# A decoder block on one Trainium2 core: RWKV's bonus sum and gate product in rounded parts instead of plain fp32, with one buffer for a pair's low-rank weights

## The chip, the cores and the metric

The kernel runs as one program on one core of a Trainium2 chip. The metric is the time of one execution in device microseconds, and smaller is better. Five engines work side by side, each through its own instructions in a fixed order: TensorE (PE in the profile; its weight loads are listed apart as PEld), VectorE (DVE), ScalarE (ACT), GpSimd (POOL) and SyncE (SP, which here only issues transfers). An instruction whose operand or buffer is not ready waits, and everything behind it on the same engine waits with it.

## The reference

The reference is one residual block: parallel RWKV-7 time mixing and sliding-window attention, merged through gates, then a gated convolutional feed-forward part, on 512 tokens of width 2048. The change touches two lines of the RWKV part:

```
g = jax.nn.sigmoid(gd) @ g2
...
y = ((y - mu) * lax.rsqrt(var + GN_EPS)).reshape(B, S, RW_DIM)
y = y * gn_w.astype(f32) + gn_b.astype(f32)
bonus = jnp.sum(rh * kh * r_k.astype(f32), axis=-1, keepdims=True) * vh
out = (y + bonus.reshape(B, S, RW_DIM)) * g.astype(f32)
```

There are 16 heads of 64. `gd` has 256 columns, so the gate product sums over 256 values for each of the 1024 columns of `g`. The bonus sums `r*k*r_k` over the 64 values of a head.

## The kernel before

**Number formats.** A matmul on fp32 tiles is called plain here. The kernel's large products avoid it: `split` (L208 to L210) makes a rounded part `hi` with ACT (`AF.Copy` into the type float32r) and a rest `lo = src - hi` with DVE. A product is then a sum of passes over such parts. The rounded weights of the projections are made the same way in `load_w` (L232 to L246): one transfer into `raw`, `whi` on ACT (L240), `wlo` on DVE (L241). Both have four buffers, and each is used by 12 passes.

**Projection passes.** `project` (L248 to L257) runs three passes for each 128 rows of the sum: `whi*xhi` (L255), `whi*xlo` (L256) and `wlo*xhi` (L257), each 128x128 by 128x512 into the PSUM tile `acc`. One `ztile` is 48 such passes. They depend on nothing in RWKV's recurrence.

**The RWKV stage.** It works on eight pairs of heads, `p` = 0 to 7. `early(p)` makes the pair's keys, values and decays out of three projection tiles. `late(p)` runs the recurrence in eight chunks (passes `psG` L731, `psU` L734, `psS` L740, with copies between them on ACT and DVE) and then the group normalisation of `y` (DVE L758 to L765; its rsqrt is `rsqrt_small`, tiles `rg`, L193 to L200, thirteen small operations of which all but one use the one before). `final(p)` transposes `y` (L772), copies it back with ACT (L778), scales it, adds the bonus, multiplies by the gate product and stores it. The program calls `late(p)`, `early(p+1)`, `final(p)` and then three `emit_gate` projections. A scheduler then places the instructions of each engine by their dependences, so the projection passes of the next pair and of the gates stand between the passes of the recurrence. They are called fillers below.

**The two places of the change.** In `early(p)`, L589 makes `rk`, L591 multiplies it by the matrix `bo` (ones where two rows belong to the same head, zeros elsewhere) in one plain matmul, and L593 makes `bon` from the result. In `final(p)`, `lora(ps, ag, 1, 1 + NG)` runs two plain matmuls at L534, and L783 multiplies their sum into `yc`. The third use of `lora`, for `a2` in `early(p)`, is also listed under L534. `wl` (L537) holds a pair's low-rank weights in two buffers: 128 columns for the decay, 128 for `a2`, 256 for the gate. `ads` holds the right-hand sides of all `lora` products. PSUM results of all these products use the tag `bulk` with three buffers.

Of the kernel before, what the change touches and what calls it, by code (L numbers as in the profile page):

```python
# [8 lines left out]
F32 = mybir.dt.float32  # L9
F32R = mybir.dt.float32r  # L10
# [3 lines left out]
ALU = mybir.AluOpType  # L14
# [4 lines left out]
P = 128  # L19
S = 512  # L20
# [114 lines left out]
def block_kernel(ctx: ExitStack, tc: tile.TileContext, d: Dims, a: dict, out: bass.AP):  # L135
    nc = tc.nc
    act, dve, pool, pe, sync = nc.scalar, nc.vector, nc.gpsimd, nc.tensor, nc.sync
# [37 lines left out]
    K = {nm: cst[:, o - P : o - P + n] for nm, (o, n) in CONST_AT.items() if o}  # L175
# [7 lines left out]
    def col(nm, i=0):  # L183
        return pcol[:, PR[nm] + i : PR[nm] + i + 1]

    def rsqrt_small(pl, ss, scale, eps, mx=None, tag="rq"):
        n = ss.shape[-1]
        tl = [pl.tile([P, 8], F32, name=f"{tag}{i}", tag=f"{tag}{i}", bufs=2)[:, :n] for i in range(3)]
        v, y, t = tl
        if mx is not None:  # L190
            dve.tensor_scalar(v, ss, mx, None, op0=ALU.max)
        else:
            dve.tensor_scalar(v, ss, scale, eps, op0=ALU.mult, op1=ALU.add)  # L193
        dve.tensor_scalar(t.bitcast(I32), v.bitcast(I32), 1, None, op0=ALU.logical_shift_right)
        dve.tensor_scalar(y.bitcast(I32), t.bitcast(I32), -1, 0x5F3759DF, op0=ALU.mult, op1=ALU.add)
        dve.tensor_scalar(v, v, -0.5, None, op0=ALU.mult)
        for _ in range(3):
            dve.tensor_tensor(t, y, y, op=ALU.mult)
            dve.tensor_tensor(t, t, v, op=ALU.mult)
            dve.scalar_tensor_tensor(y, t, 1.5, y, op0=ALU.add, op1=ALU.mult)  # L200
        return y
# [6 lines left out]
    def split(hi, lo, src, pin=free):  # L208
        pin(act.activation(hi, src, AF.Copy))
        pin(dve.tensor_tensor(lo, src, hi.bitcast(F32) if hi.dtype == F32R else hi, op=ALU.subtract))  # L210
# [67 lines left out]
    if True:  # L278
# [3 lines left out]
        with tc.tile_pool(name="x0_ps", bufs=6, space=PSUM) as ps0:  # L282
            ssum = p0.tile([P, NT], F32, name="ssum")
            HT = NT // 2
            for h in range(2):
# [3 lines left out]
                r = rsqrt_small(p0, ssum[:, h * HT : (h + 1) * HT], 1.0 / d.D, RMS_EPS)  # L289
# [3 lines left out]
            for h in range(2):  # L293
                hs = slice(h * HT * P, (h + 1) * HT * P)
                for k in range(NK):
                    ps = ps0.tile([P, HT * P], F32, name="ps_x", tag="x")
# [45 lines left out]
        with ExitStack() as pt:  # L342
# [4 lines left out]
            def small():  # L347
                return mps.tile([P, S], F32, name="mi", tag="mi")
# [26 lines left out]
            for t in range(NKV):  # L375
# [12 lines left out]
                ps = small().rearrange("p (n c) -> p n c", c=P)  # L388
                for b in range(NT):
                    pe.transpose(ps[:, b], vf[:, b * P : (b + 1) * P], ident)  # L390
                ps = ps.rearrange("p n (h c) -> p n h c", c=HD)
# [14 lines left out]
            for g in range(NHK):  # L406
# [7 lines left out]
                for n in range(NT):  # L414
# [11 lines left out]
                    for h in range(GQ):  # L426
                        slope = float(2.0 ** (-8.0 * (g * GQ + h + 1) / d.HQ))
                        dve.scalar_tensor_tensor(sc[:, h, k0:], K["dist"][:, k0:], slope, scp[h % 2][:, h // 2, k0:],
                                                 op0=ALU.mult, op1=ALU.add)
# [17 lines left out]
                    for kb in kbs:  # L447
                        ps = small().rearrange("p (h c) -> p h c", c=P)
# [3 lines left out]
                    ps = small()  # L452
                    for kb in kbs:
                        for i in range(2):
                            pe.matmul(ps, vhl[:, n - 1 + kb, g].rearrange("p e c -> p (e c)"),
                                      phl[i][:, kb].rearrange("p h c -> p (h c)"),
                                      start=kb == kbs[0] and i == 0, stop=kb == kbs[-1] and i == 1)
                    ol = ap_.tile([HD, S], F32, name="ol", tag="ol", bufs=2)
                    act.activation(ol, ps[HD:P], AF.Copy)
                    ps, ol = (x[0:HD].rearrange("p (e j c) -> p e j c", e=2, c=P) for x in (ps, ol))  # L460
# [6 lines left out]
        with ExitStack() as pr:  # L467
            lp = pr.enter_context(tc.tile_pool(name="lora", bufs=1, reuse_waits="tile"))
            zp_ = pr.enter_context(tc.tile_pool(name="zpad", bufs=1, reuse_waits="tile"))
            bd = pr.enter_context(tc.tile_pool(name="bd", bufs=1, reuse_waits="tile"))  # L470
            wk = pr.enter_context(tc.tile_pool(name="wk", bufs=1, reuse_waits="tile"))
# [17 lines left out]
            def bulk():  # L489
                return blk.tile([P, S], F32, name="bulk", tag="bulk")  # L490

            NG = d.GL // P
            thw = lp.tile([P, S], F32, name="thw")
            ads = lp.tile([P, 1 + NG, S], F32, name="ads")
            acc = ztile(d.c_wd)
            shifted(acc, PR["muwd"], thw, 0)
            act.activation(thw, thw, AF.Tanh)
# [1 line left out]
                dve.memset(thw[d.DL : P], 0.0)  # L499
            dve.memset(thw[d.DL : d.DL + 1], 1.0)  # L500
            acc = ztile(d.c_ad)
            adz = ads[:, 0]
            shifted(acc, PR["muad"], adz, 1)
            if d.AL < P:
                dve.memset(adz[d.AL : P], 0.0)
            for i in range(NG):
                acc = ztile(d.c_gd + i * P)
                t = wtile("lw")
                shifted(acc, PR["mugd"] + i, t, i % 2)
                act.activation(t, t, AF.Tanh, scale=0.5)  # L510
                dve.tensor_scalar(ads[:, 1 + i], t, 0.5, 0.5, op0=ALU.mult, op1=ALU.add)

            HV = ((0, C), (C, P))

# [14 lines left out]
            def r3(ap, c=C):  # L529
                return ap.rearrange("p (n c) -> p n c", c=c)  # L530

            def lora(ps, w, lo, hi):
                for i in range(lo, hi):
                    pe.matmul(ps, w[:, i], ads[:, i], start=i == lo, stop=i == hi - 1)  # L534

            def early(p):
                wl = lp.tile([P, 2 + NG, P], F32, name="wl", tag="wl", bufs=2)  # L537
                sync.dma_start(wl, a["lora"][p].rearrange("p (k c) -> p k c", c=P))
                w2, ag = wl[:, 0], wl[:, 1:]

                acc = ztile(d.c_k + p * P)
                kz = wtile("kz")
                shifted(acc, PR["mu"] + NP + p, kz, 0)
                kk = wtile("kk")
                dve.tensor_scalar(kk, kz, col("k_k", p), None, op0=ALU.mult)
                sq = wtile("lg")
                act.activation(sq, kk, AF.Square)
                ps = bulk()
                head_stats(ps, sq)
                rs = rsqrt_small(wk, ps[:, 0 : 2 * NT], None, None, mx=1e-24)  # L550
                rb = head_rows(wk, bulk(), rs, "lg")
                dve.tensor_tensor(kk, kk, rb, op=ALU.mult)


                ps = bulk()
                for t in range(NT):
                    ts = slice(t * P, (t + 1) * P)
                    pe.matmul(ps[:, ts], thw[:, ts], w2, start=True, stop=True)
                lg = wtile("lw")
                act.activation(lg, ps, AF.Tanh, scale=0.5)  # L560
                dve.tensor_scalar(lg, lg, 1.0, None, op0=ALU.add)
                ps = bulk()
                for t in range(NT):
                    ts = slice(t * P, (t + 1) * P)
                    pe.matmul(ps[:, ts], lg[:, ts], K["tri"], start=True, stop=True)
                act.activation(Et[:, :, 1:], r3(ps), AF.Exp, scale=-0.5 * SQE)
                Ei = wtile("Ei")
                act.activation(Ei, ps, AF.Exp, scale=0.5 * SQE)

                ps = bulk()  # L570
                lora(ps, ag, 0, 1)
                ta = wtile("lw")
                act.activation(ta, ps, AF.Tanh, scale=0.5, bias=half[:, 0, p : p + 1])

                acc = ztile(d.c_r + p * P)
                rz = wtile("rz")
                shifted(acc, PR["mu"] + p, rz, 1)
                acc = ztile(d.c_v + p * P)
                vz = wtile("vz", 2)
                shifted(acc, PR["mu"] + 2 * NP + p, vz, 0)  # L580

                k2 = wtile("k2")
                dve.tensor_scalar(k2, ta, half[:, 1, p : p + 1], half[:, 2, p : p + 1], op0=ALU.mult, op1=ALU.add)
                dve.tensor_tensor(k2, k2, kz, op=ALU.mult)
                dve.tensor_scalar(ta, ta, 0.5, 0.5, op0=ALU.mult, op1=ALU.add)
                kb = kz
                dve.tensor_tensor(kb, kk, ta, op=ALU.mult)
                rk = wtile("lw")
                dve.scalar_tensor_tensor(rk, rz, col("r_k", p), k2, op0=ALU.mult, op1=ALU.mult)  # L589
                ps = bulk()  # L590
                pe.matmul(ps, K["bo"], rk, start=True, stop=True)  # L591
                bon = wtile("bon", 2)
                dve.tensor_tensor(bon, vz, ps, op=ALU.mult)  # L593
                return ag, Ei, kk, kb, k2, rz, vz, bon
# [173 lines left out]
            def final(p, st):  # L768
                ag, bon, y = st
                ps = bulk().rearrange("p (t c) -> p t c", c=P)  # L770
                for t in range(NT):
                    pe.transpose(ps[:, t], y[:, t * P : (t + 1) * P], ident)  # L772
                yc = wtile("gn")
                dst = yc.rearrange("p (t w c) -> p t w c", w=2, c=C)
                for w, (rl, rh) in enumerate(HV):
                    for h, (lo, hi) in enumerate(HV):
                        ol, oh = HV[1 - h]
                        act.activation(dst[lo:hi, :, w], ps[rl:rh, :, ol:oh], AF.Copy)  # L778
                dve.tensor_scalar(yc, yc, col("gn_w", p), col("gn_b", p), op0=ALU.mult, op1=ALU.add)
                dve.tensor_tensor(yc, yc, bon, op=ALU.add)  # L780
                ps = bulk()
                lora(ps, ag, 1, 1 + NG)
                dve.tensor_tensor(yc, yc, ps, op=ALU.mult)  # L783
                pool.dma_start(o_rw_d[p], yc)

# [80 lines left out]
    with ExitStack() as pbb:  # L866
# [8 lines left out]
        for m, i in order:  # L875
            hi, lo, r0, n, gi = parts[i]
# [11 lines left out]
            if second:  # L888
                w = min(XC, d.D)
                for e in range(m * XC, (m + 1) * XC, w):  # L890
                    t, c0 = divmod(e, d.D)
# [494 lines left out]
```

## Time and profile before

| | before |
|---|---|
| median of 3 runs | 2829.64 us (2828.12 to 2833.07) |
| profiled execution, its time | 2830.7 us |
| span of the profiled execution | 2828.9 us |
| granted TensorE clock, mean | 0.996 |
| instructions in the span | 45923 |
| HBM read and written | 554.38 MB and 174.40 MB |

The profiled execution's time is 1.8 us more than its span, which runs from the first to the last instruction. It lies 1.06 us above the median, inside the three runs. The RWKV stage runs from about 300 to 1110 us.

A row of the timeline begins with its start and its duration, both in microseconds. A bracket at the end gives the idle time before it and what ended that. Matmuls overlap, and their ends are modelled, so the distance between starts is what a pass takes in a dense row, not its duration. One plain matmul is recorded as two.

### The profile page before, as it was taken

The page shows a single profiled execution, that of the slowest core. Times are in us where ns is not written, and L with a number is a line of the kernel's source. Part 1 is how long each engine was busy: PE and PEld are TensorE (multiplying, and loading weights), DVE is VectorE, ACT ScalarE, POOL GpSimd, SP SyncE. Part 2 cuts the span into 40 slices and gives each one's busy share as a digit, 9 for nine tenths or more (in the row PEclk, how much of TensorE's full clock was granted, in tenths as well). Part 3 has the DMA queues.
Part 4 walks back from the last instruction along what each step waited for, and adds up shares of the span by engine and source line. Part 5 has one row for each costly group of instructions (what it writes and reads, how often), then busy time and mean ns, then how long its engine had stood idle before and what let it go on. Part 6 is the DMA issues. An engine that isn't in the chain of part 4 may idle for free.

```text
span 2828.9 us, 45923 instructions
## 1 busy us (share of the span) xinstructions
PE 2774.4 (98%) x17450; PEld 2403.0 (85%) x17450; DVE 1987.5 (70%) x3437; ACT 1342.1 (47%) x2256; POOL 225.1 (8%) x299
## 2 busy tenths in 40 slices
PE   7999999999999999999999899999999999999999
PEld 5777777777777777888888899999999999888887
DVE  4588677777777774545678777878787878655555
ACT  4355445444544553322465455555545555444444
POOL 0001000000000001011010011011101110000000
PEclk9999999999999999999999999999999999999999
DMA  7865766666666667878777789888988897877775
GB/s 216 227 159 163 187 167 168 175 164 158 175 162 171 160 165 223 234 248 292 237 251 211 210 235 241 229 229 227 241 236 222 228 242 228 315 245 241 256 256 190
DMA packets 223726, 607.04 MB, mean 215 GB/s; under 512 B 24448, under 2 KB 44560, under 8 KB 222480
## 3 DMA queue, kind: packets, MB, share of 16 engines
q1 hardware_dynamic: 156096, 432.64, 47.1%
q0 software_dynamic: 36064, 132.14, 24.5%
q10 hardware_dynamic: 31344, 39.31, 4.0%
q8 instruction: 137, 2.24, 0.3%
q14 instruction: 85, 0.70, 0.1%
HBM read 554.38 MB, written 174.40 MB: 258 GB/s over the span
## 4 chain that ended last, share of the span: by engine, by line
PE 87%; DVE 5%; ACT 3%; DMA 2%; issue 1%; SPq 0%; POOL 0%; ACTq 0%; DVEq 0%; POOLq 0%
PE X L1087 18%; PE X L954 11%; PE acc L256 9%; PE acc L255 9%; PE acc L257 9%; PE Y L954 9%; PE Y L1087 9%; PE Z L1087 4%; DVE wlo L241 1%; PE psS L740 1%; PE psG L731 1%; PE bulk L623 1%; PE bulk L673 1%; PE bulk L534 1%; ACT whi L240 1%
## 5 line engine op out<-in xcount | busy, mean ns | idle before, releaser
L255 PE MATMUL acc<-xhi,whi 128*128 128x512 f32 x1152 | 462.9, 402 | 1.9 <-DVE xlo L301 1.9
L257 PE MATMUL acc<-xhi,wlo 128*128 128x512 f32 x1152 | 463.8, 403 | 0.0
L256 PE MATMUL acc<-xlo,whi 128*128 128x512 f32 x1152 | 462.2, 401 | 0.0
L947 DVE TENSOR_TENSOR wlo<-raw,whi 128x1024 fp32r<-128x1024 f32 x210 | 256.9, 1224 | 205.1 <-ACT whi L946 204.9
L240 ACT ACTIVATE whi<-raw 128x512 fp32r<-128x512 f32 x352 | 220.0, 630 | 375.7 <-PE acc L256 295.1
L946 ACT ACTIVATE whi<-raw 128x1024 fp32r<-128x1024 f32 x210 | 222.8, 1061 | 290.6 <-PE X L954 152.9
L241 DVE TENSOR_TENSOR wlo<-raw,whi 128x512 fp32r<-128x512 f32 x352 | 241.3, 689 | 167.1 <-ACT whi L240 146.9
L1087 PE MATMUL X<-b,whi 128*128 128x256 f32 x1472 | 270.2, 284 | 2.3 <-DVE u L1107 0.9
L1087 PE MATMUL X<-t,whi 128*128 128x256 f32 x1408 | 259.6, 285 | 10.3 <-DVE u L1107 9.8
L1070 DVE TENSOR_TENSOR wlo<-raw,whi 128x1024 fp32r<-128x1024 f32 x176 | 215.0, 1222 | 77.6 <-ACT whi L1069 77.3
L1087 PE MATMUL Y<-t,whi 128*128 128x256 f32 x1408 | 257.1, 283 | 0.0
L255 PEld LDWEIGHTS acc<-xhi,whi 128*128 128x128 f32 x1152 | 217.6, 189 | 43.4 <-issue 2.5
L256 PEld LDWEIGHTS acc<-xlo,whi 128*128 128x128 f32 x1152 | 217.5, 189 | 41.9 <-issue 3.3
L257 PEld LDWEIGHTS acc<-xhi,wlo 128*128 128x128 f32 x1152 | 217.5, 189 | 38.3 <-issue 1.1
L1069 ACT ACTIVATE whi<-a 128x1024 fp32r<-128x1024 f32 x132 | 139.3, 1056 | 216.5 <-DVE a L1063 214.3
L1087 PEld LDWEIGHTS X<-b,whi 128*128 128x128 f32 x1472 | 230.7, 193 | 3.1 <-issue 2.4
L1087 PEld LDWEIGHTS X<-t,whi 128*128 128x128 f32 x1408 | 221.6, 194 | 10.9 <-DVE u L1107 7.2
L1087 PEld LDWEIGHTS Y<-t,whi 128*128 128x128 f32 x1408 | 219.8, 192 | 0.0
L1087 PE MATMUL X<-b,wlo 128*128 128x256 f32 x736 | 209.3, 284 | 2.1 <-DVE wlo L1070 2.1
L1070 DVE TENSOR_TENSOR wlo<-a,whi 128x1024 fp32r<-128x1024 f32 x132 | 161.7, 1226 | 67.3 <-ACT whi L1069 66.7
L1087 PE MATMUL X<-t,wlo 128*128 128x256 f32 x704 | 200.4, 285 | 0.0
L1087 PE MATMUL Y<-t,wlo 128*128 128x256 f32 x704 | 199.4, 283 | 0.0
(339 smaller groups left out, 5762.1 us busy)
## 6 DMA issues: line engine op xcount, KB each, us to landing
raw<-in_w_up_dram SPq DMA_DIRECT2D x180, 512.0 KB, 4.6
raw<-in_w_z_dram SPq DMA_DIRECT2D x288, 256.0 KB, 3.9
s_dn<-in_w_dn_dram POOLq DMA_DIRECT2D x88, 512.0 KB, 5.9
raw<-in_w_up_dram POOLq DMA_DIRECT2D x88, 512.0 KB, 8.7
raw<-s_dn SPq DMA_DIRECT2D x88, 512.0 KB, 3.8
raw<-in_w_dn_dram SPq DMA_DIRECT2D x66, 512.0 KB, 3.5
a<-in_w_up_dram SPq DMA_DIRECT2D x48, 512.0 KB, 6.9
s_dn<-in_w_dn_dram SPq DMA_DIRECT2D x44, 512.0 KB, 4.9
```

What stands on the lines that cost most here:

```text
L240: act.activation(hi, raw, AF.Copy)
L241: dve.tensor_tensor(lo, raw, hi.bitcast(F32), op=ALU.subtract)
L255: pe.matmul(acc, whi[:, j], xhi[:, k], start=first, stop=False)
L256: pe.matmul(acc, whi[:, j], xlo[:, k], start=False, stop=False)
L257: pe.matmul(acc, wlo[:, j], xhi[:, k], start=False, stop=last)
L534: pe.matmul(ps, w[:, i], ads[:, i], start=i == lo, stop=i == hi - 1)
L946: act.activation(whi, wr, AF.Copy)
L947: dve.tensor_tensor(wlo, wr, whi.bitcast(F32), op=ALU.subtract)
L954: pe.matmul(dst, l[:, q, ts], r[:, es], start=fst and j == 0, stop=lst and j == 2, skip_group_check=True)
L1069: pin(act.activation(hi, t, AF.Copy))
L1070: pin(dve.tensor_tensor(lo, t, hi.bitcast(F32), op=ALU.subtract))
L1087: pin(pe.matmul(ps, l[:, k], r[:, k], start=start and k + i == 0, stop=last and i == 2, skip_group_check=True))
```

## The change

The bonus product is taken as two passes over float32r tiles. `rk` is split into two parts, `bo` is copied once into a float32r tile `bor`, and the two parts are multiplied one after the other into the same PSUM tile. The tiles for the parts are the existing work tiles with the tags `lg` (rounded part) and `gn` (rest), one buffer each. The first also holds `sq` and `rsb` in `early`, the second the squares in `late` and `yc` in `final`.

The gate product is taken as six passes in place of two plain matmuls: for each of the two halves of 128, rounded by rounded, rounded weights by the rest of the data, rest of the weights by rounded data. The data side (`gdhi`, `gdlo`) is split once ahead of the pairs. The weight side (`wghi`, `wglo`, two buffers each) is split in every `early`. With that, `wl` has one buffer. `ads` is gone, and the `a2` product stays plain, with `adz` and `wl[:, 1]`.

```diff
@@ -491,7 +491,10 @@
             thw = lp.tile([P, S], F32, name="thw")
-            ads = lp.tile([P, 1 + NG, S], F32, name="ads")
+            adz = lp.tile([P, S], F32, name="adz")
+            gdz = [lp.tile([P, NG, S], F32R, name=f"gd{e}") for e in ("hi", "lo")]
+            bor = lp.tile([P, P], F32R, name="bor")
+            dve.tensor_copy(bor, K["bo"])
...
-                dve.tensor_scalar(ads[:, 1 + i], t, 0.5, 0.5, op0=ALU.mult, op1=ALU.add)
+                dve.tensor_scalar(t, t, 0.5, 0.5, op0=ALU.mult, op1=ALU.add)
+                split(gdz[0][:, i], gdz[1][:, i], t)
...
-            def lora(ps, w, lo, hi):
-                for i in range(lo, hi):
-                    pe.matmul(ps, w[:, i], ads[:, i], start=i == lo, stop=i == hi - 1)
-
             def early(p):
-                wl = lp.tile([P, 2 + NG, P], F32, name="wl", tag="wl", bufs=2)
+                wl = lp.tile([P, 2 + NG, P], F32, name="wl", tag="wl", bufs=1)
                 sync.dma_start(wl, a["lora"][p].rearrange("p (k c) -> p k c", c=P))
-                w2, ag = wl[:, 0], wl[:, 1:]
+                w2 = wl[:, 0]
+                ag = [lp.tile([P, NG, P], F32R, name=f"w{e}", tag=f"w{e}", bufs=2) for e in ("ghi", "glo")]
+                split(*ag, wl[:, 2:])
...
-                lora(ps, ag, 0, 1)
+                pe.matmul(ps, wl[:, 1], adz, start=True, stop=True)
...
+                rkl = [wk.tile([P, S], F32R, name=f"rk{e}", tag="gn" if e else "lg") for e in range(2)]
+                split(*rkl, rk)
                 ps = bulk()
-                pe.matmul(ps, K["bo"], rk, start=True, stop=True)
+                for e in range(2):
+                    pe.matmul(ps, bor, rkl[e], start=e == 0, stop=e == 1)
...
                 ps = bulk()
-                lora(ps, ag, 1, 1 + NG)
+                for i in range(NG):
+                    for j, (l, r) in enumerate(((0, 0), (0, 1), (1, 0))):
+                        pe.matmul(ps, ag[l][:, i], gdz[r][:, i], start=i + j == 0, stop=i == NG - 1 and j == 2)
                 dve.tensor_tensor(yc, yc, ps, op=ALU.mult)
```

The scheduler moves instructions. Three places matter below, all shown for a pair in the middle of the stage.

On PE, beside the last but four `psS` of a pair, the plain bonus product (L591 before) gives way to the first of the two passes (L595, `rk` by `bor`). Before:

```order
L257 MATMUL acc<-xhi,wlo 128x512
L255 MATMUL acc<-xhi,whi 128x512
L591 MATMUL bulk<-lw,cst 128x512
L740 MATMUL psS<-UV,W_2913 128x64 x2
L256 MATMUL acc<-xlo,whi 128x512
L257 MATMUL acc<-xhi,wlo 128x512
```

With the change:

```order
L257 MATMUL acc<-xhi,wlo 128x512
L255 MATMUL acc<-xhi,whi 128x512
L256 MATMUL acc<-xlo,whi 128x512
L257 MATMUL acc<-xhi,wlo 128x512
L255 MATMUL acc<-xhi,whi 128x512
L595 MATMUL bulk<-rk_5155,bor 128x512
L744 MATMUL psS<-UV,W_2921 128x64 x2
L256 MATMUL acc<-xlo,whi 128x512
```

Three fillers have moved ahead of the product. Its second pass is not here: it stands behind the 28th filler after the pair's last `psS`.

On DVE, at the end of `late`, the rsqrt of the group normalisation (tiles `rg`) stood without anything between. Before:

```order
L193 TENSOR_SCALAR rg_4804<-st 128x8
L194 TENSOR_SCALAR rg_4806<-rg_4804 128x8
L195 TENSOR_SCALAR rg_4805<-rg_4806 128x8
L196 TENSOR_SCALAR rg_4804<-rg_4804 128x8
L198 TENSOR_TENSOR rg_4806<-rg_4805 128x8
L199 TENSOR_TENSOR rg_4806<-rg_4806,rg_4804 128x8
L200 SCALAR_TENSOR_TENSOR rg_4805<-rg_4806,rg_4805 128x8
L198 TENSOR_TENSOR rg_4806<-rg_4805 128x8
L199 TENSOR_TENSOR rg_4806<-rg_4806,rg_4804 128x8
```

With the change:

```order
L193 TENSOR_SCALAR rg_4834<-st 128x8
L210 TENSOR_TENSOR rk_5156<-lw,rk_5155 128x512
L194 TENSOR_SCALAR rg_4836<-rg_4834 128x8
L195 TENSOR_SCALAR rg_4835<-rg_4836 128x8
L196 TENSOR_SCALAR rg_4834<-rg_4834 128x8
L198 TENSOR_TENSOR rg_4836<-rg_4835 128x8
L199 TENSOR_TENSOR rg_4836<-rg_4836,rg_4834 128x8
L597 TENSOR_TENSOR bon<-vz,bulk 128x512
L200 SCALAR_TENSOR_TENSOR rg_4835<-rg_4836,rg_4835 128x8
L198 TENSOR_TENSOR rg_4836<-rg_4835 128x8
L199 TENSOR_TENSOR rg_4836<-rg_4836,rg_4834 128x8
L241 TENSOR_TENSOR wlo<-raw,whi 128x512
```

The rest of `rk` (L210), `bon` (L597, which stood beside an `SV` update of the recurrence before) and one `wlo` that stood in front of the next pair's first masks now stand inside the chain of the rsqrt.

On PE, at the start of `final`, before:

```order
L255 MATMUL acc<-xhi,whi 128x512
L256 MATMUL acc<-xlo,whi 128x512
L257 MATMUL acc<-xhi,wlo 128x512
L772 MATMUL bulk<-ident,yc 128x128 x4
L534 MATMUL bulk<-ads,wl 128x512 x2
L255 MATMUL acc<-xhi,whi 128x512
```

With the change:

```order
L256 MATMUL acc<-xlo,whi 128x512
L257 MATMUL acc<-xhi,wlo 128x512
L776 MATMUL bulk<-ident,yc 128x128 x4
L788 MATMUL bulk<-gdhi,wghi 128x512
L788 MATMUL bulk<-gdlo,wghi 128x512
L788 MATMUL bulk<-gdhi,wglo 128x512
L788 MATMUL bulk<-gdhi,wghi 128x512
L788 MATMUL bulk<-gdlo,wghi 128x512
L788 MATMUL bulk<-gdhi,wglo 128x512
L255 MATMUL acc<-xhi,whi 128x512
```

Two plain matmuls have become six passes. Between the pair's last `psS` and the transposes there stood 37 fillers; now there are 43, with the second bonus pass between the 28th and the 29th. Between the gate product and the next pair's first block products (L623, now L627) there stood 18 fillers, and now there are 12.

More of the change, by code (lines that the diff above doesn't have):

```diff
@@ L501, in block_kernel @@
             acc = ztile(d.c_ad)
-            adz = ads[:, 0]
             shifted(acc, PR["muad"], adz, 1)
```

## The prediction

> **What bounds the kernel now.** I read the page first, then the busy time by stretches, then PE's own waits in the RWKV stage.
>
> ```profile
> PE 2774.4 (98%) x17450; PEld 2403.0 (85%) x17450; DVE 1987.5 (70%) x3437; ACT 1342.1 (47%) x2256; POOL 225.1 (8%) x299
> PE 87%; DVE 5%; ACT 3%; DMA 2%; issue 1%; SPq 0%; POOL 0%; ACTq 0%; DVEq 0%; POOLq 0%
> 611.38:709.33 97.95, 96.74 (x634) 77.02 (x633) 74.08 (x181) 46.87 (x104) 8.15 (x11) 1.00 0.68 167
> PE bulk L673 <- DVE XIW L210: 5.3, 13, 0.6
> PE bulk L772 <- DVE yc L765: 1.8, 8, 0.2
> PE bulk L623 <- DVE bon L593: 1.6, 1, 1.6
> ```
>
> PE is busy 98% of the span and carries 87% of the chain of waits. The third row is one pair of the RWKV stage, between two equal points of the program: 97.95 us, of which PE is busy 96.74, DVE 74.08 and ACT 46.87, at full granted clock (1.00). The last rows are PE's waits from 290 to 1110 us (total, times, longest): 8.7 us for eight pairs. So PE's own work sets this stage, and a microsecond taken from it shows in the total unless it turns into a wait. Two of the three waits lie at places that the change touches.
>
> **PE's passes.** What a plain product takes is read from the chain of waits, and what a pass over rounded parts takes from the distance of two fillers, twelve passes apart, in PE's timeline.
>
> ```profile
> 692.92 0.86 PE bulk L591 x2
> 717.21 1.72 PE bulk L534 x4
> 615.28 0.39 PE L257 MATMUL acc<-xhi,wlo 128*128 128x512 f32 x1
> 618.00 0.39 PE L257 MATMUL acc<-xhi,wlo 128*128 128x512 f32 x1
> L534 PE MATMUL bulk<-ads,wl x48: 592/592/596, 312.9 to 1105.6; 128*128 128x512 f32 x48
> L591 PE MATMUL bulk<-lw,cst x16: 590/592/596, 328.3 to 987.0; 128*128 128x512 f32 x16
> ```
>
> The bonus product occupies PE for 0.86 us, the gate product for 1.72. A filler takes (618.00 - 615.28) / 12 = 0.227 us, its weight load included. The new passes have the shape and type of fillers, so I cost them as fillers. Gate: 1.72 - 6 x 0.227 = 0.36 us less per pair. Bonus: 0.86 - 2 x 0.227 = 0.41 less. Each matmul is two records, so the 16 records of L591 are one product for each of eight pairs. L534's 48 records are 24 products, of which 16 belong to the gate; the other eight stay plain. PE saves 8 x (0.36 + 0.41) = 6.1 us.
>
> **The added splits.** Prices by shape come from the same two operations elsewhere.
>
> ```profile
> L210 DVE TENSOR_TENSOR rlo<-rin,rhi x8: 683/687/695, 1123.8 to 1156.8; 128x512 fp32r<-128x512 f32 x8
> L210 DVE TENSOR_TENSOR XIW<-tt,XIW x56: 404/426/427, 339.1 to 1063.2; 128x256 f16<-128x256 f32 x56
> L209 ACT ACTIVATE rhi<-rin x8: 616/619/632, 1122.8 to 1155.9; 128x512 fp32r<-128x512 f32 x8
> L209 ACT ACTIVATE XIW<-tt x56: 407/417/419, 338.6 to 1062.8; 128x256 f16<-128x256 f32 x56
> ```
>
> A pair gains one of each shape on each engine: DVE 0.69 + 0.43 = 1.1 us, ACT 0.62 + 0.42 = 1.0. That makes about 75 of 98 us on DVE and 48 on ACT, so capacity covers them, and they cost only where they stand in a chain that PE waits for. The splits of `gd` and the copy of `bo` run once, among fillers ahead of the first pair; the same reason holds there, and I take nothing.
>
> **The chain into the transposes.** This is the place that decides. PE's timeline around the end of a pair, then DVE's:
>
> ```profile
> 609.24 0.66 PE L740 MATMUL psS<-UV,W 128*128 128x64 f32 x4
> 610.03 0.39 PE L255 MATMUL acc<-xhi,whi 128*128 128x512 f32 x1
> 618.62 0.66 PE L772 MATMUL bulk<-ident,yc 128*128 128x128 f32 x4 [0.23 <-DVE yc L765]
> 614.85 0.68 DVE L241 TENSOR_TENSOR wlo<-raw,whi 128x512 fp32r<-128x512 f32 x1
> 615.44 0.16 DVE L193 TENSOR_SCALAR rg<-st 128x8 f32<-128x8 f32 x1
> 615.64 0.17 DVE L194 TENSOR_SCALAR rg<-rg 128x8 int32<-128x8 int32 x1
> 615.85 0.17 DVE L195 TENSOR_SCALAR rg<-rg 128x8 int32<-128x8 int32 x1
> 615.93 0.17 DVE L196 TENSOR_SCALAR rg<-rg 128x8 f32<-128x8 f32 x1
> 617.87 0.69 DVE L765 TENSOR_TENSOR yc<-yc,rg 128x512 f32<-128x512 f32 x1
> ```
>
> The filler that starts at 610.03 is the second after the last `psS`, the one at 618.00 the 37th; PE is free again at 618.23 and starts the transposes at 618.62, so it really loses 0.39 us there (0.23 by the modelled ends). The transposes start 0.75 us after L765.
>
> On DVE three operations now stand inside the rsqrt. A dependent small one follows its predecessor by 0.20 us (615.44 to 615.64), an independent one by 0.08 (L195 to L196), and behind a 0.68 us operation the next starts after 0.59 (614.85 to 615.44). So an independent large one between two dependent small ones costs 0.08 + 0.60 - 0.20 = 0.48 us. Three cost 1.44: the transposes can start at 618.62 + 1.44 = 620.06. PE meanwhile has 6 more fillers and the second bonus pass: 618.23 + 7 x 0.227 = 619.82. One more wait stands between: that pass is reached at 610.03 + 27 x 0.2277 = 616.18 (0.2277 being the spacing over these 35 fillers), while the rest of `rk` starts at about 615.44 + 0.10 and ends at 616.23, so PE loses about 0.1 and is free at 619.92. It waits 0.14 for the transposes, with the 0.1 together 0.24, against 0.39 before: 0.15 less per pair, which seven pairs have (the last has no next `early`), 1.1 us in all. The bounds: if each of the three costs its whole duration of 0.69 with nothing overlapped, the chain ends 0.63 later and PE loses 0.87 instead of 0.24, which is 0.48 more than before, 3.4 us for seven pairs. If nothing were inserted as the chain sees it, PE would lose nothing at all, 2.7 us to the good. I take the 0.15, since the spacings stand in this very chain.
>
> [...]
>
> What stands behind the moved instructions: `bon` on DVE now waits for the second bonus pass, which ends at 616.28 + 0.39 = 616.67, while DVE comes to `bon` at 616.84, so it does not wait. The `wlo` behind it needs its `whi`:
>
> ```profile
> 616.84 0.63 ACT L240 ACTIVATE whi<-raw 128x512 fp32r<-128x512 f32 x1 [2.09 <-PE acc L256]
> ```
>
> That ends at 617.47, some 0.3 later with the change, and DVE comes to the `wlo` at about 617.95. Covered by 0.2 us; if not, DVE and the chain are late by what is missing.
>
> **The moved first bonus pass.** Three fillers and a pass take 0.91 us where L591 took 0.86, so `psS` behind it stays where it was. `bon` no longer stands in front of an `SV` update, a `wlo` does instead, at the same 0.60. Nothing.
>
> **The wl transfer.** With one buffer it must wait until the pair's `a2` product has read the weights. It stands behind the second `rsb` transfer's row of SP:
>
> ```profile
> 684.65 0.86 PE bulk L534 x2
> 685.21 0.52 SPq L230 DMA_DIRECT2D s_dn<-in_w_dn_dram  x1
> 693.10 6.56 SPq L237 DMA_DIRECT2D raw<-in_w_z_dram  x3
> ```
>
> The product ends at 685.51, the transfer ahead is issued by 685.73, and the next `raw` goes out at 693.10 only. Its wait has 7 us of cover, and its reader comes some 30 us later. Nothing.
>
> **The first pair.** Here both bonus passes follow each other, and PE already waits for `bon` to free a PSUM buffer.
>
> ```profile
> 333.14 1.13 PE L623 MATMUL bulk<-BAR,BKK 128*128 128x256 f32 x4 [1.60 <-DVE bon L593]
> 332.41 0.68 DVE L593 TENSOR_TENSOR bon<-vz,bulk 128x512 f32<-128x512 f32 x1
> ```
>
> DVE gets the rest of `rk` and a `wglo` in front of `bon`: 0.60 + 0.34 = 0.94 us later. Two fillers have moved ahead of the waiting product, 0.45. So this pair loses 0.5 us here, and the 0.41 that its bonus product saves only lengthens the wait: 0.9 worse than the sum of passes. Between nothing (if DVE has slack there) and 0.9, I take 0.9.
>
> **The sum.** 6.1 + 1.1 - 0.9 = 6.3 us less. It is made on the profiled execution, 2830.7 us (span 2828.9), which lies 1.06 above the median. The stages behind are bound by PE as well, so I carry it to the median: 2829.64 - 6.3 = 2823.3. What this measurement can tell from no change is about 0.2%, 5.7 us, so my forecast stands just beyond that edge.
>
> **Rivals.**
>
> *The chain gives it back.* The three insertions cost their full duration, or the `wlo` and `bon` wait for a few tenths. For it: the chain into L765 already ends PE's wait in all eight pairs. Against it: the overlap in the rows. Instead of gaining 1.1, the seven pairs lose 3.4: 6.1 - 0.9 - 3.4 = 1.8 less, 2827.8.
>
> *The new wait of bon closes a ring.* DVE stands at `bon` until PE has done the second bonus pass, and the `wlo` that PE's fillers need stands behind it. If PE ran out of rounded weights ahead of that pass, it would lose a whole turn of the ring of 12 passes, 12 x 0.227 = 2.7 us per pair: 7 x 2.7 = 19 more, 2829.64 - 6.3 + 19 = 2842. It decides, against the whole gain, from 6.3 / 7 = 0.9 us of lateness per pair on, and makes the kernel measurably slower from (6.3 + 5.7) / 7 = 1.7. For it: ACT makes each `whi` only when PE frees the buffer (2.09 us of waiting above). Against it: four buffers, three groups or 8 us ahead of PE.
>
> *The passes do not take less.* If the rounding left a pass at the 0.43 us of one record of a plain product (1.72 / 4), eight passes would take 3.44 instead of 2.58 per pair, 7 us more: 2836. The fillers with the same types speak against it.
>
> **Chances and range.** Forecast 0.58, giving back 0.29, the ring 0.08, passes of the old length 0.05. The forecast's own range is 2820.8 to 2824.7: from the chain's best bound and a first pair that loses nothing (1.6 + 0.9 less) to two tenths more per pair (1.4 more). The range for 8 in 10 takes that in and reaches over the second case: 2820.5 to 2830. The 0.2% edge is 2829.64 - 5.66 = 2824.0. Of the forecast's 0.58 some 0.48 lie beyond it, of the second case 0.02, and the two slower cases lie beyond the other edge: faster 0.50, same 0.37, slower 0.13.
>
> **What will show it.** Eight L595 and L788 passes per pair at the spacing of fillers; a pair of about 97.1 us between equal points; PE's wait at L776 for L769 at some 0.1 us and none over 0.2 at the second L595; the wait at L627 in the first pair grown from 1.6 to about 2.5 us; no wait of `raw` behind `wl`. The forecast is wrong if L769 starts more than 1.6 us later behind the last `psS` than L765 did, or if L597 waits for PE.

## The result and the profile after

| | before | after |
|---|---|---|
| median of 20 runs each on one chip, us | 2829.92 (2825.96 to 2833.54) | 2824.97 (2820.93 to 2827.93) |
| profiled execution, us (span) | 2830.7 (2828.9) | 2823.84 (2822.0) |
| a pair of the RWKV stage, us | 97.95 | 97.13 |

The ratio is 0.9981, with a 95% interval of 0.9975 to 0.9987: 4.95 us less (3.7 to 7.1). The interval lies wholly below 1, so the kernel is faster, by a little less than the 0.2% that the prediction named as the edge of what can be told from no change.

The page of the changed kernel, the busy row and the chain by engine; then the busy time by stretches for one pair between equal points, and PE's waits from 290 to 1110 us (total, times, longest), without the one behind `XIW`, which is 5.4 in total:

```profile
PE 2768.1 (98%) x17466; PEld 2401.8 (85%) x17466; DVE 1994.0 (71%) x3456; ACT 1350.7 (48%) x2274; POOL 225.3 (8%) x299
PE 88%; DVE 5%; ACT 2%; DMA 2%; issue 1%; ACTq 0%; SPq 0%; DVEq 0%; POOLq 0%
```

```profile
615.33:712.46 97.13, 96.15 (x636) 77.17 (x635) 74.78 (x183) 47.83 (x106) 8.16 (x11) 1.00 0.69 170
```

```profile
PE bulk L627 <- DVE BAR L610: 1.8, 1, 1.8
PE bulk L627 <- DVE bon L597: 1.5, 1, 1.5
PE bulk L776 <- DVE yc L769: 0.2, 1, 0.2
```

PE's busy time fell by 6.3 us (2774.4 to 2768.1), and it still sets the end. A pair is 0.82 us shorter. The wait ahead of the transposes (1.8 us over eight pairs before) is listed in one pair only, the last. In the first pair one wait of 1.6 has become two, of 1.8 for `BAR` and 1.5 for `bon`; the prediction had named one wait for `bon`, grown to about 2.5.

The end of a steady pair in PE's timeline. The columns are start, duration, engine, line, operation:

```profile
608.31 0.66 PE L744 MATMUL psS<-UV,W 128*128 128x64 f32 x4
...
615.02 0.39 PE L257 MATMUL acc<-xhi,wlo 128*128 128x512 f32 x1
615.33 0.50 PE L595 MATMUL bulk<-rk,bor 128*128 128x512 f32 x1
615.66 0.39 PE L255 MATMUL acc<-xhi,whi 128*128 128x512 f32 x1
...
618.88 0.39 PE L257 MATMUL acc<-xhi,wlo 128*128 128x512 f32 x1
619.15 0.66 PE L776 MATMUL bulk<-ident,yc 128*128 128x128 f32 x4
619.56 0.48 PE L788 MATMUL bulk<-gdhi,wghi 128*128 128x512 f32 x1
619.88 0.39 PE L788 MATMUL bulk<-gdlo,wghi 128*128 128x512 f32 x1
```

From the last `psS` to the transposes it takes 619.15 - 608.31 = 10.84 us, where it took 9.38; the prediction's own points (620.06 against 609.24) make 10.82. PE starts them 0.27 after the last filler, against a usual spacing of 0.23: it loses 0.04 there, not 0.39. The second bonus pass and the filler ahead of it take 0.64 together (615.02 to 615.66) instead of 0.46: 0.18 lost, where 0.1 was expected. The gate's first pass follows the short transposes and takes 0.32 until the next one, not 0.23.

The rsqrt chain on DVE with its three insertions:

```profile
614.52 0.17 DVE L193 TENSOR_SCALAR rg<-st 128x8 f32<-128x8 f32 x1
614.59 0.69 DVE L210 TENSOR_TENSOR rk<-lw,rk 128x512 fp32r<-128x512 f32 x1
615.19 0.17 DVE L194 TENSOR_SCALAR rg<-rg 128x8 int32<-128x8 int32 x1
...
615.88 0.68 DVE L597 TENSOR_TENSOR bon<-vz,bulk 128x512 f32<-128x512 f32 x1
616.48 0.16 DVE L200 SCALAR_TENSOR_TENSOR rg<-rg,rg 128x8 f32<-128x8 f32 x1
...
617.00 0.69 DVE L241 TENSOR_TENSOR wlo<-raw,whi 128x512 fp32r<-128x512 f32 x1
617.61 0.16 DVE L200 SCALAR_TENSOR_TENSOR rg<-rg,rg 128x8 f32<-128x8 f32 x1
...
618.40 0.69 DVE L769 TENSOR_TENSOR yc<-yc,rg 128x512 f32<-128x512 f32 x1
```

L193 to L769 takes 3.88 us, against 2.43 before (615.44 to 617.87): 1.45 for three, 0.48 each. Each large operation is followed by the next 0.60 to 0.61 us later, though it lasts 0.68 to 0.69; no idle time is listed ahead of `bon` or of the `wlo`, so neither waited.

### The profile page after: what moved, and what is told of

The parts are those of the page before. It is cut to its first block, busy times and chain, and to the rows that moved or that the text cites. A ratio compares the mean times of both kernels' runs of the same rounds, so it can differ in the third digit from the quotient of the medians.

```text
span 2822.0 us, 45987 instructions
## 1 busy us (share of the span) xinstructions
PE 2768.1 (98%) x17466; PEld 2401.8 (85%) x17466; DVE 1994.0 (71%) x3456; ACT 1350.7 (48%) x2274; POOL 225.3 (8%) x299
## 4 chain that ended last, share of the span: by engine, by line
PE 88%; DVE 5%; ACT 2%; DMA 2%; issue 1%; ACTq 0%; SPq 0%; DVEq 0%; POOLq 0%
PE X L1093 17%; PE X L960 11%; PE acc L256 10%; PE acc L255 10%; PE acc L257 10%; PE Y L960 9%; PE Y L1093 8%; PE Z L1093 4%; PE psS L744 1%; PE psG L735 1%; PE bulk L627 1%; DVE wlo L241 1%; PE bulk L677 1%; DMA raw<-in_w_dn_dram 1%; ACT whi L240 1%
```

## The experiments

Nine more runs were made, two of them of the unchanged kernels. The first four share a chip and 33 runs of the kernel before (2829.94 us). Single executions of one kernel spread over 8 to 11 us, so the verdicts rest on distances within the traces. Theory A is the forecast: PE's own passes set a steady pair. In the first pair of the changed profile I had found `kk` 1 us later than the prediction allows for (rows below), and wanted its cause.

**wl behind other loads.**

```diff
+                acc = ztile(d.c_k + p * P)
...
-                sync.dma_start(wl, a["lora"][p].rearrange("p (k c) -> p k c", c=P))
+                with tc.issue_after(wp["last"].ins):
+                    sync.dma_start(wl, a["lora"][p].rearrange("p (k c) -> p k c", c=P))
```

> The whole computation of the changed kernel; each transfer of wl is issued behind three loads of projection weights instead of next to the two rsb transfers. Theory A (the wl transfer beside rsb is what makes the first pair later than predicted): from the copy of rsT on DVE to the product of kk with rsb it takes 10.8 us as before the change (310.00 to 320.83 there, 310.25 to 322.05 in the changed kernel, which is 11.8); the waits of PE in the first pair shrink by some 1.0 us, and the total is about 1 us below the changed kernel. Theory B (the transfers of the weight sums on the other queue, which ran at the same time, made rsb late): 11.8 us stays and so does the total. Theory C: the split of wl comes too late and the weights of the projections behind it are late on ACT; the total rises. Steady pairs: 97.15 us in all of them.

Measured: 2825.79 us (ratio 0.9980, 0.9971 to 0.9988). From `rsT` to `kk` it took 12.21 us, more than in the changed kernel, and from `rsT` to the transposes of `vz` 34.2 us against 33.75. Theory A on `wl` falls: its transfer is not what delays `rsb`.

**The gate in passes alone, the bonus in passes alone.** Each edit is shown against the changed kernel, and only where the product itself is taken; the tiles and splits that it no longer needs are gone too.

```diff
-                for e in range(2):
-                    pe.matmul(ps, bor, rkl[e], start=e == 0, stop=e == 1)
+                pe.matmul(ps, K["bo"], rk, start=True, stop=True)
```

> The whole computation; the bonus sum is plain fp32 again, gate in passes and one wl buffer kept. Theory A (PE's own passes set a steady pair): the pair takes 97.93 - 0.35 = 97.6 us; PE's wait ahead of the transposes and the 9.38 us from the last psS to them stay as before, since no operation stands inside the rsqrt; rsT to kk 11.8 us. The total is 8 x 0.35 = 2.8 less than before, about 1.3 of it lost in the first pair (rsb and wglo): some 1.5 less than before. Rival (the chain on DVE sets a steady pair, and PE's passes are covered): the pair stays at 97.9.

```diff
-                for i in range(NG):
-                    for j, (l, r) in enumerate(((0, 0), (0, 1), (1, 0))):
-                        pe.matmul(ps, ag[l][:, i], gdz[r][:, i], start=i + j == 0, stop=i == NG - 1 and j == 2)
+                lora(ps, ag, 1, 1 + NG)
```

> The whole computation; the gate product is plain fp32 again with two wl buffers, the bonus sum in passes. Theory A: the pair takes 97.93 - 0.36 (passes) - 0.13 (wait ahead of the transposes) = 97.44 us; the three insertions into the rsqrt are there and cost 1.45 us of chain, which six more projection passes and the second bonus pass cover, so PE waits under 0.15 there; rsT to kk 10.8 us as before; the total is 8 x 0.36 + 7 x 0.13 - 0.6 in the first pair = 3.2 less than before. Rival (three insertions set the pair): PE waits over 0.4 at the transposes and the pair is 97.9 or more. Rival on the first pair (the rest of rk alone makes it late): the second half of the product of BKK and BAR starts as late as in the changed kernel although rsb is early.

The transposes of the first pair and of the seventh, six pairs later, in PE's timelines of the kernel before, the changed one, gate only and bonus only; the third row of the first two fences is the last pair's:

```profile
422.57 0.66 PE L772 MATMUL bulk<-ident,yc 128*128 128x128 f32 x4 [0.21 <-DVE yc L765]
1010.40 0.66 PE L772 MATMUL bulk<-ident,yc 128*128 128x128 f32 x4 [0.24 <-DVE yc L765]
1103.83 0.66 PE L772 MATMUL bulk<-ident,yc 128*128 128x128 f32 x4 [0.19 <-DVE yc L765]
```

```profile
424.80 0.66 PE L776 MATMUL bulk<-ident,yc 128*128 128x128 f32 x4
1007.71 0.66 PE L776 MATMUL bulk<-ident,yc 128*128 128x128 f32 x4
1099.51 0.65 PE L776 MATMUL bulk<-ident,yc 128*128 128x128 f32 x4 [0.20 <-DVE yc L769]
```

```profile
423.53 0.66 PE L771 MATMUL bulk<-ident,yc 128*128 128x128 f32 x4 [0.23 <-DVE yc L764]
1009.49 0.66 PE L771 MATMUL bulk<-ident,yc 128*128 128x128 f32 x4 [0.23 <-DVE yc L764]
```

```profile
422.62 0.66 PE L777 MATMUL bulk<-ident,yc 128*128 128x128 f32 x4
1008.18 0.66 PE L777 MATMUL bulk<-ident,yc 128*128 128x128 f32 x4
```

A pair takes 97.97, 97.15, 97.66 and 97.59 us on average. Gate alone saves 0.31 and leaves the wait ahead of the transposes (0.23 in its rows); bonus alone saves 0.38 and takes that wait away; both together save 0.82. The rival that DVE's chain sets a pair wanted 97.9 in both, and falls. Bonus only missed its 97.44 by 0.15, and the two gains add up to 0.69, not 0.82. A pair of an unchanged kernel differs by as much from profile to profile (by the same transposes in the second profiles below: 98.15 before, with one pair of 98.74, and 97.18 after), so how the 0.82 divides between gate and bonus is known to about 0.1 only. The totals are 2829.53 us (0.9996, 0.9987 to 1.0005) and 2826.22 (0.9988, 0.9979 to 0.9997). Gate only gained a microsecond less than expected in the middle of its interval; its first pair, below, says where. In bonus only, `wl` has two buffers and goes out early, and still `rsT` to `kk` took 11.72 us.

**The first pair's bonus sum plain.**

```diff
...
+                if not p:
+                    pe.matmul(ps, K["bo"], rk, start=True, stop=True)
-                for e in range(2):
+                for e in range(2 if p else 0):
```

> The whole computation; the bonus sum of pair 0 alone is plain fp32, the other seven in passes, gate in passes, one wl buffer. Theory A (the rest of rk stands in the way of the first pair's bon, the plain product's longer time only fills a wait): PE's waits in the first pair shrink by about 0.6 us, steady pairs 97.15, the total about 0.3 to 0.6 us below the changed kernel. Rival (the late kk alone sets the first pair): nothing comes back and the total is the same or 0.4 above.

Measured: 2826.08 us (0.9985, 0.9976 to 0.9993), no gain. DVE's work from `kk` to `bon` shrank by 0.62 us as reckoned, and still the first pair's transposes of `vz` came 1.0 us later after `kk` than in the changed kernel. That was in neither theory. PE's timeline and the busy time by stretches (length, PE busy, granted clock, DMA share, GB/s) of gate only, which did the same:

```profile
332.66 2.61 PE L622 MATMUL bulk<-BAR,BKK 128*128 128x256 f32 x8 [1.93 <-DVE bon L592]
342.95 0.66 PE L660 MATMUL bulk<-ident,vz 128*128 128x128 f32 x4
```

```profile
330.49:333.90 3.41, 1.48 (x8) 1.00 0.83 165
333.90:337.31 3.41, 3.41 (x10) 0.50 0.90 346
```

Behind a wait of 1.93 us PE's granted clock is 0.50 for 3.41 us. The eight matmul records take 2.61 us instead of 2.0 (3.23 with the plain first bonus, after the same 1.93), and the transposes of `vz` come 11.0 us after `bon` in both kernels, not the 9.42 of the changed one. I took the length of the wait for the cause; that is Theory E of the next expectations. The section on the hardware shows that length alone does not decide.

**Both kernels again.** Neither profile had been repeated, so I ran before and after a second time, unchanged.

> The kernel before, unchanged, profiled a second time. In the four kernels so far it took 11.4 to 12.2 us from the copy of rsT to the product of kk with rsb, whether wl stood beside rsb or not, against 10.8 in the one profile of the kernel before. Theory D (these two DMA steps vary from execution to execution, and the first profile of before drew a short one): it takes 11.2 us or more here, without any change of the kernel, and PE's wait for bon in the first pair is longer than 1.6. Theory A' (the change makes rsb late): it takes 10.8 again. Steady pairs 97.95.

> The changed kernel, unchanged, profiled a second time. Theory D: from rsT to kk it takes another time than 11.8, anywhere between 10.8 and 12.2; the DVE work from kk to bon takes 12.53 again, 0.95 more than the 11.58 of before, as predicted. Theory E (a wait of PE of 1.9 us or more in the first pair halves the granted clock for the next microseconds): if one of PE's two waits there is 1.9 or longer, the product of BKK and BAR behind it takes 2.6 to 3.3 us per half instead of 2.0; if both are under 1.8, it takes 2.0. Steady pairs 97.15.

DVE's timeline of the kernel before, first and second profile, and of the changed kernel:

```profile
310.00 0.27 DVE L332 COPY rsT<-bulk 8x128 f32<-8x128 f32 x1
320.83 0.69 DVE L552 TENSOR_TENSOR kk<-kk,rsb 128x512 f32<-128x512 f32 x1 [3.70 <-DMA rsb<-rsd]
```

```profile
310.00 0.27 DVE L332 COPY rsT<-bulk 8x128 f32<-8x128 f32 x1
322.10 0.69 DVE L552 TENSOR_TENSOR kk<-kk,rsb 128x512 f32<-128x512 f32 x1 [5.11 <-DMA rsb<-rsd]
333.68 0.68 DVE L593 TENSOR_TENSOR bon<-vz,bulk 128x512 f32<-128x512 f32 x1
```

```profile
310.25 0.27 DVE L332 COPY rsT<-bulk 8x128 f32<-8x128 f32 x1
322.05 0.69 DVE L553 TENSOR_TENSOR kk<-kk,rsb 128x512 f32<-128x512 f32 x1 [4.82 <-DMA rsb<-rsd]
334.58 0.68 DVE L597 TENSOR_TENSOR bon<-vz,bulk 128x512 f32<-128x512 f32 x1
```

PE's first transposes of `vz`, in the first profile of before and of the changed kernel:

```profile
342.01 0.66 PE L661 MATMUL bulk<-ident,vz 128*128 128x128 f32 x4
344.00 0.66 PE L665 MATMUL bulk<-ident,vz 128*128 128x128 f32 x4
```

The same kernel took 10.83 us from `rsT` to `kk` in one execution and 12.10 in the other; the changed one 11.80 and 11.69. Theory D holds: the two DMA steps vary by over a microsecond, and the first profile of before drew the shortest of the eleven. The part of Theory D that wanted a longer wait for `bon` in the second profile of before missed: that wait was 1.60 again, and a wait of 1.09 for `BAR` stood ahead of it. From `kk` to `bon`, DVE takes 11.58 us in both profiles of before (332.41 and 333.68) and 12.53 and 12.54 in those of after. In the second profile of after the waits were 1.62 and 1.48 and both halves took 2.0 us. The second profiles came out at 2834.3 and 2821.97 us: such is the spread of one execution.

**The gate passes twice.**

```diff
+                for _ in range(2):
-                for i in range(NG):
+                    for i in range(NG):
```

> The changed kernel with the six gate passes of a pair run twice into the same sum buffer, the second time from a fresh start: work is added, none left out. Theory A (PE's own passes set a pair, and one takes 0.227 us): a pair takes 97.15 + 6 x 0.227 = 98.51, the whole kernel 8 x 1.36 = 10.9 us more than the changed kernel, 2836. Rival (the chain on DVE sets a pair and PE has slack): a pair stays within 0.3 of 97.15 and the kernel at 2825 to 2828.

Measured: 2836.38 us (1.0018, 1.0009 to 1.0027). The changed kernel's median comes from other runs of the kernel before; by the two ratios this is some 10.5 us more than the changed kernel. In PE's timeline:

```profile
425.04 0.66 PE L776 MATMUL bulk<-ident,yc 128*128 128x128 f32 x4
1015.93 0.66 PE L776 MATMUL bulk<-ident,yc 128*128 128x128 f32 x4
```

A pair takes 98.48 us, 1.33 more: 0.222 for each added pass. PE sets the pair, and a pass costs what a filler costs.

**First pair: split of rk and bonus product behind the block products.** The edit makes the split and the product a function `bonus`, and issues `wl` late as in the first experiment:

```diff
+                if p:
+                    bonus()
...
+                if not p:
+                    bonus()
                 dve.tensor_tensor(BKK, BKK, ee.unsqueeze(2).to_broadcast([P, NCH, P]), op=ALU.mult)
```

> The whole computation; the changed kernel with, in the first pair alone, the split of rk and the bonus product put behind the product of BKK and BAR, and with each wl transfer behind three loads of projection weights. Theory (DVE is never idle from kk to bon in the first pair, so PE's first wait there ends later by each operation in front of the last BAR): the last BAR comes 0.6 us earlier after kk, 8.2 instead of 8.76 us, and PE's first wait shrinks by 0.6 for the same time from rsT to kk; the second wait moves to the last quarter of the product and stays about as long, since three wlo, a wglo and vz stand in front of AB as before. About 0.5 us less than the changed kernel in the first pair, 2 us less where a halved clock is avoided; steady pairs 97.15. Rival: the second wait grows by what the first loses, and nothing is gained.

Measured: 2825.70 us (0.9979, 0.9970 to 0.9988). PE's waits in the first pair are 1.6 us for `BAR` and 1.7 for the W product. The last `BAR` came 0.63 us earlier after `kk` (7.44 instead of 8.07; the expectation had named the end of the operation). But PE was there earlier too, since the two bonus passes no longer stood ahead, and the rest went into the second wait: `kk` to the transposes of `vz` took 21.99 us, against 21.95. The rival was right.

**vz twice in the first pair.** A deliberate wait for Theory E.

```diff
+                if not p:
+                    m = PR["mu"] + 2 * NP
+                    dve.scalar_tensor_tensor(vz, acc, omu[:, m : m + 1], zpads[0][:, 0:S], op0=ALU.mult, op1=ALU.add)
```

> The changed kernel with vz of the first pair computed twice, the second time between the AB and the W product ahead of bon: work is added, none left out. bon starts 0.66 + 0.33 = 0.99 us later after kk (13.5 instead of 12.53), two more projection passes stand ahead of the second half of the product of BKK and BAR, so PE's second wait there grows from 1.46 to about 1.46 + 0.99 - 0.45 = 2.0. Theory E (a wait of 1.9 us or more halves the granted clock behind it): the second half takes 2.6 to 3.3 us instead of 2.0 and the fillers behind it are slow too, so the transposes of vz on PE start about 11.0 us after bon instead of 9.42, unless the first wait had been over 1.9 and the clock had already dropped there. Rival (the slow halves in three kernels had another cause): 2.0 us, and the transposes 9.0 to 9.4 us after bon.

Inconclusive: 2824.99 us in one run, and the wait it was to make did not come about. The buffer that PE waited for was now freed by the W product, which stood ahead of `bon`, and both waits of the first pair were 1.5 us.

No kernel beat the changed one by more than the measurement can tell.

## Why the prediction was right, point by point

- **PE bounds the stage: right.** Added passes cost their whole time (gate twice, 0.222 us each), saved ones come back (gate only 0.31 us per pair, bonus only 0.38).
- **The passes, 6.1 us: right in kind, a little too large.** From the transposes to the second filler behind the gate product it takes 2.44 us before (618.62 to 621.06) and 2.11 after (619.15 to 621.26), so the gate saves 0.33 us, not 0.36. Of a pair's 0.82 the gate and the wait below (0.13) leave 0.36 for the bonus, not 0.41: 8 x 0.69 = 5.5. I costed all eight passes as fillers among fillers; the gate's first pass takes 0.32 behind the transposes. Why the bonus saves less was not followed up.
- **The chain into the transposes, +1.1: right.** Three insertions cost 1.45 us, against 1.44 predicted, and moved fillers cover them. PE loses 0.04 + 0.18 instead of 0.39, so 0.13 to 0.17 is gained per pair; with 0.13, 7 x 0.13 = 0.9. The prediction's upper price, 0.69 for each insertion with nothing overlapped, was not met: in these rows the next operation starts 0.60 to 0.61 us after one of 0.68 to 0.69.
- **The first pair, -0.9: right in size, not in form.** `bon` comes 12.53 - 11.58 = 0.95 later after `kk` (0.94 predicted). The transposes of `vz` come 21.95 us after `kk` where they came 21.15 (the mean of two profiles: 342.01 - 320.83 and 343.23 - 322.10). With two fillers done earlier (0.45) and 0.36 of bonus time not realised, that is 0.80 - 0.45 + 0.36 = 0.7. But the wait for `bon` did not grow. The rest of `rk` stands in front of the last `BAR` already, which comes 8.07 us after `kk` instead of 7.44, and PE waits 1.78 us for that one first. The prediction had followed `bon` alone. What looked like another microsecond was the DMA draw of the first profile of before.
- **bon, the ring, raw behind wl: right.** No wait of `bon` or of the `wlo` behind it; no wait of a `raw` behind `wl` is listed in the steady pairs.

The measured terms make 5.5 + 0.9 - 0.7 = 5.7 us. A check without them: from `kk` of the first pair to the last transposes it is 783.00 us before and 777.46 after, 5.5 less, and the last gate product behind them saves another 0.3. The medians say 4.95, with 3.7 to 7.1. So the term that was mis-sized is the price of the passes: they save 0.69 us per pair, where the prediction had 0.77. The first pair is a few tenths the other way. A gain of 5.7 us is the 0.2% edge itself, so "faster" against "same" was near even. What remains, 0.8 us between traces and medians, is within the interval and was not followed up. The profiled executions differ by 6.9 us, about 2 of it behind this stage, where nothing was changed; from 1500 to 1600 us the granted clock was 0.93 on average in the profile of before and 0.97 in that of after.

## What the runs showed of the hardware

In the first pair PE's waits of 1.93 us (gate only, first bonus plain) and 2.13 (`wl` later, gate twice) are each followed by a clock of 0.50; those of 1.78 and below are not. That looks like a matter of the wait's length, and Theory E took it so. A later stage, where nothing was changed, speaks against it: in the two profiles of the changed kernel PE waits 2.77 and 2.76 us at one place there, and behind it the clock stays at 1.00 in the first and is 0.50 in the second. PE's timeline and its time by stretches in the first and in the second, the stretches as long as the slow one of gate only:

```profile
1532.57 0.47 PE L1093 MATMUL X<-t,whi 128*128 128x256 f32 x2 [2.77 <-DVE u L1113]
1527.91:1531.32 3.41, 1.89 (x16) 1.00 0.89 171
1531.32:1534.74 3.42, 2.17 (x18) 1.00 0.37 133
1534.74:1538.15 3.41, 2.94 (x24) 1.00 0.50 68
```

```profile
1532.13 0.77 PE L1093 MATMUL X<-t,whi 128*128 128x256 f32 x2 [2.76 <-DVE u L1113]
1528.21:1531.62 3.41, 1.16 (x10) 1.00 0.44 159
1531.62:1535.03 3.41, 2.90 (x13) 0.50 0.32 28
```

In the first profile PE is busy for 1.89 and 2.17 us of the two stretches of 3.41 and 3.42 us that the wait lies across, in the second for 1.16 of the 3.41 us that hold most of it. In gate only it was 1.48 of 3.41 us in the stretch ahead of the slow one. So the length of a wait alone does not decide, and the same kernel met the slow clock there in one execution and not in the other. What does decide is not shown: PE was busy for less in the two stretches that the slow clock followed, but these are a few cases, and no run varied the busy time on purpose.

Where the slow stretch fell ahead of another wait it cost nothing: with `wl` later, the first half of the block products takes 3.32 us behind a wait of 2.13, but the second wait vanishes and the transposes of `vz` come 9.42 us after `bon`, as in the changed kernel. Where it fell behind the last wait it cost 1.5 to 1.6 us (gate only, first bonus plain): there 0.34 us of DVE work in front of `bon` took a wait of 1.60 to 1.93. All in all the clock was 0.50 behind a wait of 1.93 us (gate only), and stayed at 1.00 behind one of 2.77 (changed kernel, first profile).

## What to carry to other kernels

In this kernel, with PE busy 98% of the time, an added pass cost 0.222 us, about its spacing among fillers (0.227), but the gate's first pass, behind the short transposes, took 0.32: read both from the timeline. Three insertions into DVE's dependent chain cost the spacings shown in that chain, 0.48 us each, and as movable work covered them, PE lost only 0.04 us ahead of the transposes. Before you explain a microsecond between two profiles, profile the unchanged kernel twice: here two DMA steps took 10.83 us in one execution of it and 12.10 in the other. What a wait of PE costs may depend on what follows it: the slow clock behind one cost 1.5 to 1.6 us in two kernels here and nothing in a third. Read the granted clock behind a wait before you price it.
